# Hybrid mLSTM / Hyena / attention trunk: up projections accumulated over a bank that ScalarE filled, and adaLN chunks moved between engines and stages

## The chip, the cores and the metric

One NeuronCore of a Trainium2 chip runs the whole program once. The metric is the device time of one execution in microseconds (us), as the median of several runs. Engines are named as in the profile: PE is TensorE's matmul, PEld its weight load, DVE is VectorE, ACT is ScalarE, POOL is GpSimd, SP is the engine whose queue issues nearly all DMAs.

## What is computed

The reference is one inference step of a two-layer trunk on 512 latent tokens and 128 context tokens, D_MODEL = 1024, FF = 2816, float32. Cut to what the change touches:

```python
def adaln(cvec, w, b):                       # six chunks of 1024: shift, scale, gate; shift, scale, gate
    return jnp.split((jax.nn.silu(cvec) @ w + b)[:, None, :], 6, axis=-1)

def conv_ffn(h, w_up, w_conv, w_down):
    a, g = jnp.split(h @ w_up, 2, axis=-1)
    return (jax.nn.gelu(dwconv3(a, w_conv)) * g) @ w_down

for l in range(2):                           # l = 0: mixer A + B; l = 1: mixer C (attention)
    sh1, sc1, gt1, sh2, sc2, gt2 = adaln(c, w_ada[l], b_ada[l])
    x = x + gt1 * mixer(rmsnorm(x, g_mix[l]) * (1 + sc1) + sh1)
    x = x + gt2 * conv_ffn(rmsnorm(x, g_ffn[l]) * (1 + sc2) + sh2, w_up[l], w_conv[l], w_down[l])
```

Chunks are numbered 0 to 5 in the order of that list. Chunk 2 of a layer is first needed by the residual of its output projection, chunks 3 and 4 by the second norm, chunk 5 by the residual of its down projection.

## The kernel before

The activations lie transposed in SBUF, features on the 128 partitions and 640 tokens (512 latent, 128 context) along the free axis, as eight tiles of 128 features. A float32 matrix product is made of three fp32r matmuls: each operand is split into a high part (an ACT copy) and a low part (a DVE subtraction). The 640 tokens go in two halves of 320 (HT). So every weight that is loaded (a `raw` tile, four slots) costs an ACT copy and a DVE subtraction before PE can use it (`load_w` and `split_w`, lines 99 to 112; `split_half`, line 512).

The order of the stages is mixer A and B (`mixer_ab`), the output projection of layer 0 (`out_proj`, line 1152) with the second norm hidden in its last three tiles, the feed-forward network of layer 0 (`ffn_s`, line 414), mixer C (`mixer_c`, line 1179), the output projection of layer 1, its feed-forward network, and a last norm. A scheduler in the framework fixes the order of each engine's queue at compile time from its own model of times; at run time each queue is in order. `tc.issue_after(ins)` puts instructions behind a named one on its engine.

**The feed-forward network.** Chunks f = 0 to 2 of the 22 chunks of 128 features go through a plain product. From f = 3 on, `up(f)` (line 528) forms both halves of the up projection with seven products of a Winograd form instead of eight. Each product is 12 matmuls of 320 columns over four k-tiles; their weights are called w1 to w7 in the code. The seven products collect in three PSUM banks A, B and C: w1 then w2 in A; w6, w7, w4 in B; w5, w3 in C. The product w1 is needed by four results: once in A itself, and three times added to B. For this, ACT copies A to an SBUF tile `s1` (line 538), and three times DVE adds `s1` to B on its way out, to `u2`, `u3` and `gg`. Two chunks overlap: PE's order is w1 of the new chunk, w4 of the old one, w6 of the new, w3 of the old, then w2, w7, w5 of the new. After up(5), up(10) and up(15) a down projection (`down`, line 585) of the chunks up to then is made: eight output tiles, each with its weight split and with a residual in three pieces on DVE (line 360). The last down projection follows at the end.

**The adaLN chunks.** There are two ways to make one. `ada_pe` (line 212) makes a chunk, or two halves, on PE: four steps, each with two DMAs of 512 KB and 4 fp32 matmuls of 32 x 512 packed beside each other in the array (8 instructions in the trace), then one ACT copy, 4 tiny fp32 products with `selc` (8 instructions), and two DVE additions. `ada_dve` (line 242) makes it on DVE: 16 steps, each with a DMA of 256 KB (`adw`) and two multiply-and-sum instructions (`adj`, line 254), each followed by a read of the accumulator; at the end two small additions. Before the change layer 0's chunks 0 and 1 are made by `ada_pe` at the start, 2 to 5 by `ada_pe` in mixer A and B, one step after each of 16 projection tiles. Layer 1's chunks 0, 1, 2 are made by `ada_dve` in the feed-forward network of layer 0: the `filler` of `down` issues two steps after each output tile, with two `adw` buffers, so the 48 steps fill the first three down projections. Layer 1's chunks 3, 4, 5 are made by `ada_dve` in mixer C, six steps in each of the eight head pairs, with one `adw` buffer.

Of the kernel before, what the change touches and what calls it, by code (L numbers as in the profile page):

```python
# [17 lines left out]
P = 128  # L18
D = 1024
KT = 8  # L20
# [17 lines left out]
def trunk(ctx: ExitStack, tc: tile.TileContext, I, O, dbg=None, stop=None):  # L38
# [173 lines left out]
    def ada_pe(l, blocks, pl, tag, bufs, sbp, sbt):  # L212
        nm = "".join(f"{ch}{half}" for ch, half in blocks)
        pt = pst(f"ada{nm}")
        for kp in range(4):
            rr = [pl.tile([P, 1024], F32, tag=tag, name=f"wa{nm}{kp}{i}", bufs=bufs) for i in range(2)]
            for i, (ch, half) in enumerate(blocks):
                sp.dma_start(out=rr[i], in_=I["w_ada"][ch, kp, half])
            for par in range(2):
                for i in range(2):  # L220
                    j = 2 * par + i
                    pe.matmul(pt[32 * j : 32 * j + 32, :], cs_[0][:, 2 * kp + par, :],  # L222
                              rr[i][:, par * 512 : (par + 1) * 512], start=(kp == 0), stop=(kp == 3))
            if kp < 3:
                yield
# [16 lines left out]
    def ada_dve(l, ch, pl, bufs, cb):  # L242
# [20 lines left out]
        return [lambda k=k, h=h: step(k, h) for k in range(KT) for h in range(2)]  # L263

# [149 lines left out]
    def ffn_s(l, pools, early, steps, mk_hook):  # L414
# [7 lines left out]
        def filler(st=None):  # L422
            every[0] += 1
            st = steps if st is None else st
            for _ in range(2):
# [102 lines left out]
        def up(f):  # L528
# [8 lines left out]
            s1 = fp.tile([P, HT], F32, tag="s1", name=f"s1{l}_{f}")  # L537
            act.copy(out=s1, in_=A[:, :HT])
# [5 lines left out]
            B = pst(f"B{l}_{f}")  # L544
            product(B, split_half(a11, f"w6{f}"), T2, True, True)
            u2 = fp.tile([P, HT], F32, tag="u2", name=f"u2{l}_{f}")
            tt(u2, B[:, :HT], s1, ALU.add)
# [8 lines left out]
            tt(u3, B[:, :HT], s1, ALU.add)  # L556
# [7 lines left out]
            tt(gg[:, 0:HT], B[:, :HT], s1, ALU.add)  # L564
# [28 lines left out]
        for f in range(NC, NF):  # L593
# [5 lines left out]
            filler(early)  # L599
# [116 lines left out]
    def mixer_ab():  # L716
        with ExitStack() as es:
            es_h = es.enter_context(ExitStack())
            csil = es_h.enter_context(tc.tile_pool(name="cs", bufs=1, side="right")).tile([P, KT, 32], F32, name="csil")
            dve.memset(csil, 0.0)  # L720
            act.activation(out=csil[:, :, 0:2], in_=cond.rearrange("p s k -> p k s"), func=AF.Silu)
            cs_.append(csil)
# [77 lines left out]
            steps = [ada_pe(0, ((ch, 0), (ch, 1)), hw, "adr", 2, modp, "adasb") for ch in (2, 3, 4, 5)]  # L800
# [351 lines left out]
    def out_proj(l, src, order, hook, steps):  # L1152
        here = [None]

        def done(i, pt, a):
            here[0] = residual(l, 2, i, pt, a)

        def filler():
            for _ in range(2):
                if steps:  # L1160
                    with tc.issue_after(here[0]):
                        steps.pop(0)()

        ks = [(k, XH[:, k], XL[:, k]) for k in order]
        n = 0
        if psum["shape"] != (3, 2):
            linear([src[0], src[1]], done, f"oq{l}", ks=ks, by_half=False, filler=filler)
# [11 lines left out]
    def mixer_c():  # L1179
        with ExitStack() as es:  # L1180
# [3 lines left out]
            steps = [q for ch in (3, 4, 5) for q in ada_dve(1, ch, at, 1, cb)]  # L1184
# [112 lines left out]
            def pair_att(pr, nxt):  # L1297
# [118 lines left out]
    def layer(l, src, order, mk_hook):  # L1416
        with ExitStack() as es:
            pools = ffn_open(es, l)
            early, steps = [], []
            if l == 0:  # L1420
                cb = cond_bcast(pools[0], "cb0")
                steps = [q for ch in (0, 1, 2) for q in ada_dve(1, ch, pools[1], 2, cb)]
            with ExitStack() as en:
                nrm = en.enter_context(tc.tile_pool(name=f"nrm{l}1", bufs=2, side="right", reuse_waits="tile"))
                st = norm_steps(l, 1, nrm, pools[3])
                out_proj(l, src, order, lambda: next(st), early)
# [9 lines left out]
            ffn_s(l, pools, early, steps, hook)  # L1436
# [89 lines left out]
def pack(i):  # L1526
# [12 lines left out]
    o["w_ada"] = wa[0].reshape(4, 2, P, 6, 2, 512).transpose(3, 0, 4, 2, 1, 5).reshape(6, 4, 2, P, 1024)  # L1539
# [88 lines left out]
```

## Time and profile before

| | |
|---|---|
| runs of the kernel before | 1722.22, 1720.52, 1723.1 us; median 1722.22 us |
| the profiled execution's own time | 1722.28 us |
| its span, first to last instruction | 1720.5 us |
| mean granted TensorE clock | 0.987 of full speed |
| PE, DVE, ACT busy | 1642.9, 1300.1, 803.7 us |

The profiled execution lies 0.06 us from the median, and 1.8 us of its time lie outside its span. Busy time of PE is modelled from pipelined matmuls; idle time is listed by what ended it. A granted clock of 1.00 means 2.4 GHz, and 0.5 would mean 1.2 GHz throughout.

### The profile page before, as it was taken

How to read it: one execution, taken by the hardware profiler on the slowest of the kernel's cores; microseconds unless marked ns; L12 is line 12 of the kernel's file. 1: busy time of each engine (PE TensorE's matmuls, PEld its weight loads, DVE VectorE, ACT ScalarE, POOL GpSimd, SP SyncE). 2: the span in 40 equal slices, each digit the busy share in tenths (PEclk: the TensorE clock that was granted, in tenths of full speed). 3: DMA queues.
4: the chain of work that ended last, by engine and by line, in shares of the span. 5: the costliest groups of instructions: out<-in, count | busy, mean ns of one | idle time of the engine just before them, and what ended most of it. 6: DMA issues, size and time to landing. Idle time of an engine off the chain costs nothing.

```text
span 1720.5 us, 28571 instructions
## 1 busy us (share of the span) xinstructions
PE 1642.9 (95%) x11018; PEld 1541.3 (90%) x11018; DVE 1300.1 (76%) x2796; ACT 803.7 (47%) x1529; POOL 141.1 (8%) x158
## 2 busy tenths in 40 slices
PE   5999999999998999989998999999999999999997
PEld 2699778999998998989998889888999999999997
DVE  5887537665888989899857877778478597786974
ACT  6323226574751533425436555556266344443542
POOL 3110001000100000000020212111010000000001
PEclk9999999999999999999999999999999999999998
DMA  8334432132235333252323333332214232223221
GB/s 326 113 129 174 161 134 79 52 107 73 75 91 161 96 112 125 80 166 81 104 81 102 109 118 96 121 95 83 74 45 115 67 98 74 86 68 105 74 86 62
DMA packets 70136, 180.64 MB, mean 105 GB/s; under 512 B 8992, under 2 KB 19536, under 8 KB 69744
## 3 DMA queue, kind: packets, MB, share of 16 engines
q1 hardware_dynamic: 68176, 174.71, 33.0%
q0 software_dynamic: 1824, 4.10, 1.3%
q8 instruction: 87, 1.43, 0.3%
q14 instruction: 49, 0.40, 0.1%
HBM read 170.65 MB, written 4.20 MB: 102 GB/s over the span
## 4 chain that ended last, share of the span: by engine, by line
PE 53%; DVE 12%; DMA 5%; ACT 2%; issue 2%; POOL 0%; POOLq 0%; ACTq 0%; DVEq 0%
PE B L525 11%; PE pd L127 10%; PE C L525 7%; PE A L525 7%; DMA adw<-in_w_adaT 5%; PE pqk L127 4%; DVE adj L254 4%; PE pu L127 2%; PE pu L121 1%; PE pop L127 1%; PE pd L121 1%; PE pS L1329 1%; DVE s L1215 1%; PE py L1344 1%; PE pS L1309 1%
## 5 line engine op out<-in xcount | busy, mean ns | idle before, releaser
L360 DVE SCALAR_TENSOR_TENSOR x<-pd,mod,x 128x320 f32<-128x320 f32 (+2 forms) x192 | 75.0, 434 | 98.6 <-PE pd L127 89.0
L254 DVE CUSTOM_DVE_ANT_0 adj<-adw,cbc 128x512 bf16<-128x512 f32 x96 | 68.9, 718 | 22.8 <-DMA adw<-in_w_adaT 21.8
L254 DVE CUSTOM_DVE_ANT_0 adj<-adw,cb 128x512 bf16<-128x512 f32 x96 | 65.9, 687 | 10.5 <-DMA adw<-in_w_adaT 9.6
L575 DVE SCALAR_TENSOR_TENSOR fcb<-fca,cwf,fcb 128x641 f32<-128x641 f32 x76 | 67.0, 881 | 2.9 <-ACT fcb L573 2.6
L1331 ACT COPY pTs<-pS 128x384 f32<-128x384 f32 (+1 forms) x80 | 34.4, 434 | 36.4 <-PE pS L1329 36.0
L1317 DVE CUSTOM_DVE_ANT_0 s<-pS,bm 128x384 f32<-128x384 f32 x64 | 33.9, 548 | 18.8 <-PE pS L1316 18.6
L447 ACT ACTIVATE fcb<-fcb 128x641 f32<-128x641 f32 x44 | 32.6, 740 | 30.0 <-DVE fcb L575 30.0
L1329 PE MATMUL pS<-ident,s 128*128 128x128 f32 x208 | 36.9, 280 | 9.6 <-DVE s L1215 9.6
L530 DVE TENSOR_TENSOR u<-B,s 128x320 f32<-128x320 f32 x76 | 36.9, 486 | 12.1 <-PE B L525 11.6
L573 ACT ACTIVATE fcb<-fca,cwf 128x641 f32<-128x641 f32 x38 | 31.7, 834 | 27.3 <-DVE fca L530 26.8
L442 ACT CAST G<-gg 128x640 fp32r<-128x640 f32 x44 | 32.0, 727 | 26.5 <-DVE gg L530 22.1
L1215 DVE TENSOR_SCALAR s<-s,nm 128x384 f32<-128x384 f32 (+1 forms) x80 | 43.6, 548 | 0.8
L1213 ACT ACTIVATE s<-s,nm 128x384 f32<-128x384 f32 x64 | 39.1, 611 | 10.3 <-DVE nm L1317 9.8
L360 DVE SCALAR_TENSOR_TENSOR x<-pop,mod,x 128x320 f32<-128x320 f32 (+2 forms) x36 | 14.3, 433 | 36.7 <-PE pop L127 26.1
L288 ACT ACTIVATE sqn<-x 128x320 f32<-128x320 f32 x56 | 25.3, 466 | 33.8 <-DVE x L360 26.6
L222 PE MATMUL ada<-wa,csil 128*32 128x512 f32 x192 | 39.3, 653 | 1.5 <-DMA wa<-in_w_ada 1.3
L1394 POOL TENSOR_TENSOR fo<-fo,rs 128x320 f32<-128x320 f32 x8 | 6.9, 888 | 394.6 <-ACT rs L1386 394.6
L1329 PEld LDWEIGHTS pS<-ident,s 128*128 128x128 f32 x208 | 24.0, 141 | 16.3 <-DVE s L1215 12.3
L1292 POOL TENSOR_TENSOR bm<-amask,wr 128x768 f32<-128x768 f32 x14 | 28.7, 2052 | 115.0 <-issue 91.5
L443 DVE TENSOR_TENSOR G<-gg,G 128x640 fp32r<-128x640 f32 x44 | 36.0, 818 | 2.4 <-ACT G L442 2.3
L289 DVE TENSOR_TENSOR accn<-accn,sqn 128x320 f32<-128x320 f32 x56 | 30.7, 554 | 8.5 <-ACT sqn L288 7.6
L103 POOL TENSOR_TENSOR qk00l<-qk,qk00h 128x1024 fp32r<-128x1024 f32 x1 | 2.7, 2742 | 412.1 <-DVE rn L303 412.1
(2011 smaller groups left out, 6152.9 us busy)
## 6 DMA issues: line engine op xcount, KB each, us to landing
wa<-in_w_ada SPq DMA_DIRECT2D x48, 512.0 KB, 4.6
adw<-in_w_adaT SPq DMA_DIRECT2D x96, 256.0 KB, 3.0
d<-in_w_down SPq DMA_DIRECT2D x48, 320.0 KB, 2.9
qk<-in_w_qkv SPq DMA_DIRECT2D x24, 512.0 KB, 3.6
d<-in_w_down SPq DMA_DIRECT2D x16, 448.0 KB, 3.3
u<-in_w_up SPq DMA_DIRECT2D x12, 512.0 KB, 3.6
qk<-in_w_ab SPq DMA_DIRECT2D x8, 512.0 KB, 4.4
op<-in_w_oab SPq DMA_DIRECT2D x6, 512.0 KB, 3.7
```

Of the source, the lines that this page charges most:

```text
L121: pe.matmul(o, ww[:, kt], xx[:, c], start=False, stop=last and n == 1)
L127: pe.matmul(bank(pt, a)[:, : sp_[a][1] - sp_[a][0]], ww[:, kt], xx[:, slice(*sp_[a])], start=(first and n == 0), stop=(last and n == 2))
L222: pe.matmul(pt[32 * j : 32 * j + 32, :], cs_[0][:, 2 * kp + par, :], rr[i][:, par * 512 : (par + 1) * 512], start=(kp == 0), stop=(kp == 3))
L254: dve.tensor_tensor_reduce(out=jk, in0=w, in1=cb[:, s, c], op0=ALU.mult, op1=ALU.add, scale=1.0, scalar=0.0, accum_out=got[0][:, k, h, s : ...
L360: r = dve.scalar_tensor_tensor(out=x[:, k, c0:c1], in0=bank(pt, h)[:, c0 - h * HT : c1 - h * HT], scalar=mod[:, l, ch, k, s : s + 1], in1= ...
L443: here[0] = dve.tensor_tensor(out=g[:, 1], in0=pr, in1=g[:, 0].bitcast(F32), op=ALU.subtract).ins
L525: pe.matmul(o, ww[:, k], xx[:, k], start=(first and k == 0 and n == 0), stop=(last and k == 3 and n == 2), skip_group_check=not first)
L530: tt = lambda o, a, b, op: dve.tensor_tensor(out=o, in0=a, in1=b, op=op)
L575: dve.scalar_tensor_tensor(out=o, in0=av[:, d : d + T + 1], scalar=w[j], in1=o, op0=ALU.mult, op1=ALU.add)
L1213: act.activation(out=s, in_=src, func=AF.Exp, scale=-1.0, bias=nm, accum_out=sm)
L1215: return dve.tensor_scalar(out=s, in0=s, scalar1=sm, scalar2=None, op0=ALU.mult).ins
L1329: pe.transpose(pS[:, j * P : (j + 1) * P], s[:, j * P : (j + 1) * P], ident)
```

## The change

Three things are changed. In `up`, ACT copies the first product from bank A to bank B instead of to SBUF; the product w6 then accumulates over it, and the three results of B leave as plain ACT copies where DVE added `s1` before. Chunk 5 of each layer is made by `ada_pe` between the tiles of its own output projection (with a small `csil` tile of its own: a DVE memset and an ACT Silu; four buffers for the weights), so layer 0's mixer has three `ada_pe` chunks and 12 steps left. Of layer 1's other chunks, 0 and 1 stay in the feed-forward network of layer 0, now 32 steps, issued two and one in turn after each output tile; 2, 3 and 4 are made in mixer C, seven steps in each of the pairs 1 to 7 and none in pair 0.

```diff
 def ada_pe(l, blocks, pl, tag, bufs, sbp, sbt):
-                sp.dma_start(out=rr[i], in_=I["w_ada"][ch, kp, half])
+                sp.dma_start(out=rr[i], in_=I["w_ada"][6 * l if l else ch, kp, half])
...
+    def silu_cols(pl, nm):
+        csil = pl.tile([P, KT, 32], F32, name=nm)
+        dve.memset(csil, 0.0)
+        act.activation(out=csil[:, :, 0:2], in_=cond.rearrange("p s k -> p k s"), func=AF.Silu)
+        cs_[:] = [csil]
...
     def ffn_s(...): filler
-            for _ in range(2):
+            for _ in range(1 + every[0] % 2):
...
     def up(f):
             A = pst(f"A{l}_{f}")
             product(A, split_half(a11, f"w1{f}"), B11, True, True)
-            s1 = fp.tile([P, HT], F32, tag="s1", name=f"s1{l}_{f}")
-            act.copy(out=s1, in_=A[:, :HT])
+            B = pst(f"B{l}_{f}")
+            act.copy(out=B[:, :HT], in_=A[:, :HT])
...
-            B = pst(f"B{l}_{f}")
-            product(B, split_half(a11, f"w6{f}"), T2, True, True)
+            product(B, split_half(a11, f"w6{f}"), T2, False, True)
-            tt(u2, B[:, :HT], s1, ALU.add)
+            act.copy(out=u2, in_=B[:, :HT])
...
-            tt(u3, B[:, :HT], s1, ALU.add)
+            act.copy(out=u3, in_=B[:, :HT])
...
-            tt(gg[:, 0:HT], B[:, :HT], s1, ALU.add)
+            act.copy(out=gg[:, 0:HT], in_=B[:, :HT])
...
     def mixer_ab():
-            steps = [ada_pe(0, ((ch, 0), (ch, 1)), hw, "adr", 2, modp, "adasb") for ch in (2, 3, 4, 5)]
+            steps = [ada_pe(0, ((ch, 0), (ch, 1)), hw, "adr", 2, modp, "adasb") for ch in (2, 3, 4)]
...
             def qk_tile(j):
-                if j in (5, 3, 2, 6):
-                    filler()
...
-    def out_proj(l, src, order, hook, steps):
+    def out_proj(l, src, order, hook, ao):
+        st = ada_pe(l, ((5, 0), (5, 1)), ao, "adr", 4, ao, "adasb")
...
             use_psum(3, 2)
             n = 2
+        next(st)
         linear([src[i] for i in range(n, KT)], lambda i, pt, a: done(n + i, pt, a), f"op{l}",
-               ks=ks, head=0 if n else 3, tail=3, by_half=False, hook=hook, filler=filler)
+               ks=ks, head=0 if n else 3, tail=3, by_half=False, hook=hook, filler=lambda: next(st, 0))
...
     def mixer_c():
-            steps = [q for ch in (3, 4, 5) for q in ada_dve(1, ch, at, 1, cb)]
+            steps = [q for ch in (2, 3, 4) for q in ada_dve(1, ch, at, 1, cb)]
...
-                        if 1 <= n <= 6:
+                        if pr and 1 <= n <= 7 and steps:
...
     def layer(l, src, order, mk_hook):
-                steps = [q for ch in (0, 1, 2) for q in ada_dve(1, ch, pools[1], 2, cb)]
+                steps = [q for ch in (0, 1) for q in ada_dve(1, ch, pools[1], 2, cb)]
...
+                ao = en.enter_context(tc.tile_pool(name=f"ao{l}", bufs=1, side="right", reuse_waits="tile"))
+                silu_cols(ao, f"csil{l}")
```

## Rows read from the trace of the kernel before

**Rows 1.** The page, part 1: busy time, share of the span, instructions.
```profile
PE 1642.9 (95%) x11018; PEld 1541.3 (90%) x11018; DVE 1300.1 (76%) x2796; ACT 803.7 (47%) x1529; POOL 141.1 (8%) x158
```

**Rows 2.** Two stretches: us; busy PE, PEld, DVE, ACT, POOL; clock; DMA; GB/s.
```profile
515.30:846.50 331.20, 316.47 (x2091) 313.16 (x2089) 302.04 (x653) 130.17 (x219) 0.00 (x0) 0.97 0.39 116
1348.11:1655.00 306.89, 306.89 (x2093) 306.73 (x2092) 243.68 (x454) 130.00 (x220) 0.00 (x0) 1.00 0.30 86
```

**Rows 3.** Waits of PE, stretch 515 to 853: us in total, times, longest.
```profile
PE B L525 <- ACT w45wh L517: 5.1, 1, 5.1
PE B L525 <- ACT w415wh L517: 4.4, 1, 4.4
PE B L525 <- ACT w611wh L517: 3.9, 1, 3.9
```

**Rows 4.** Timeline around the end of layer 0's first down projection: start, duration, what.
```profile
551.61 0.69 DVE L254 CUSTOM_DVE_ANT_0 adj<-adw,cb 128x512 bf16<-128x512 f32 x1 [0.64 <-DMA adw<-in_w_adaT]
...
559.19 0.62 ACT L517 CAST w45wh<-u_6a 128x512 fp32r<-128x512 f32 x1 [2.15 <-DVE u_6a L530]
...
559.86 0.90 PE L525 MATMUL B<-TT,w45wh 128*128 128x320 f32 x2 [5.09 <-ACT w45wh L517]
...
560.29 0.68 DVE L254 CUSTOM_DVE_ANT_0 adj<-adw,cb 128x512 bf16<-128x512 f32 x1
```

**Rows 5.** Groups by line, stretch 515 to 852: busy us, mean ns | idle before.
```profile
L254 DVE CUSTOM_DVE_ANT_0 adj<-adw,cb 128x512 bf16<-128x512 f32 x96 | 65.9, 687 | 10.5 <-DMA adw<-in_w_adaT 9.6
L254 DVE DVE_READ_ACCUMULATOR2_ANT ada<- 128x1 f32 x96 | 7.8, 82 | 0.0
```

**Rows 6.** Timeline of SP's queue in layer 0's first down projection.
```profile
522.87 1.79 SPq L251 DMA_DIRECT2D adw<-in_w_adaT  x2
...
553.55 5.36 SPq L251 DMA_DIRECT2D adw<-in_w_adaT  x3
```

**Rows 7.** The page, part 5: the additions that bring s1 to u2 and u3.
```profile
L530 DVE TENSOR_TENSOR u<-B,s 128x320 f32<-128x320 f32 x76 | 36.9, 486 | 12.1 <-PE B L525 11.6
```

**Rows 8.** Groups by line, stretch 1348 to 1655: the copy of the first product.
```profile
L538 ACT COPY s<-A 128x320 f32<-128x320 f32 x16 | 6.8, 424 | 1.4 <-PE A L525 0.9
```

**Rows 9.** Timeline: first product's copy and the next products, chunks 7 and 14, layer 1.
```profile
1397.39 0.46 PE L525 MATMUL B<-TT,w17wh 128*128 128x320 f32 x2
...
1397.64 0.42 ACT L538 COPY s<-A 128x320 f32<-128x320 f32 x1
...
1399.15 0.46 PE L525 MATMUL B<-TT,w67wh 128*128 128x320 f32 x2
...
1519.49 0.42 ACT L538 COPY s<-A 128x320 f32<-128x320 f32 x1
...
1520.62 0.46 PE L525 MATMUL B<-TT,w413wh 128*128 128x320 f32 x2
```

**Rows 10.** PE in mixer A and B: one adaLN step, and the products with selc.
```profile
103.67 1.06 PE L222 MATMUL ada<-wa,csil 128*32 128x512 f32 x8
...
135.94 0.95 PE L230 MATMUL adaq<-selc,adasb 128*128 128x4 f32 x8
```

**Rows 11.** Stretch 100 to 240, the tile ada alone; columns PE, PEld, DVE, ACT.
```profile
100.00:240.00 140.00, 24.32 (x128) 3.43 (x128) 0.00 (x0) 2.14 (x4) 1.00 0.48 164
```

**Rows 12.** Timeline at layer 1's output projection: ACT's gap and PE's.
```profile
1216.29 1.05 ACT L102 CAST op11h<-op 128x1024 fp32r<-128x1024 f32 x1 [4.66 <-PE poq L127]
...
1220.13 0.52 PE L127 MATMUL pop<-XH,op10h 128*128 128x320 f32 x2 [2.70 <-DVE mod L258]
```

**Rows 13.** Timeline at layer 0's output projection: last split, PE's wait, a table load.
```profile
384.25 0.83 DVE L1175 TENSOR_TENSOR XL<-og,XH 128x640 fp32r<-128x640 f32 x1 [0.79 <-ACT XH L1174]
...
388.83 0.54 PE L127 MATMUL pop<-XH,op00h 128*128 128x320 f32 x2 [0.44 <-DVE x L360]
...
389.26 1.28 ACT L268 ACT_TABLE_LOAD   x1
```

**Rows 14.** The page, part 6: the chunk's DMAs on PE's way: count, KB, median us.
```profile
wa<-in_w_ada SPq DMA_DIRECT2D x48, 512.0 KB, 4.6
```

More of the change, by code (lines that the diff above doesn't have):

```diff
@@ L212, in ada_pe @@
     def ada_pe(l, blocks, pl, tag, bufs, sbp, sbt):
-        nm = "".join(f"{ch}{half}" for ch, half in blocks)
+        nm = str(l) + "".join(f"{ch}{half}" for ch, half in blocks)
         pt = pst(f"ada{nm}")
@@ L412, in ffn_open, with ffn_s @@
         return fc, fp, gtile, keep
-    def ffn_s(l, pools, early, steps, mk_hook):
+    def ffn_s(l, pools, steps, mk_hook):
         fc, fp, gtile, keep = pools
@@ L420, in ffn_s, with filler @@
         every = [0]
-        def filler(st=None):
+        def filler():
             every[0] += 1
-            st = steps if st is None else st
-            for _ in range(2):
+            st = steps
+            for _ in range(1 + every[0] % 2):
                 if st:
@@ L598, in ffn_s @@
                     next(s_)
-            filler(early)
             old = new
@@ L718, in mixer_ab @@
             es_h = es.enter_context(ExitStack())
[L719 to L722, printed above, removed]
+            silu_cols(es_h.enter_context(tc.tile_pool(name="cs", bufs=1, side="right")), "csil")
             modp = es.enter_context(tc.tile_pool(name="modp", bufs=1))
@@ L1150, in mixer_ab @@
             dump("ym", og)
-    def out_proj(l, src, order, hook, steps):
[L1153 to L1162, printed above, removed]
+    def out_proj(l, src, order, hook, ao):
+        st = ada_pe(l, ((5, 0), (5, 1)), ao, "adr", 4, ao, "adasb")
+        done = lambda i, pt, a: residual(l, 2, i, pt, a)
         ks = [(k, XH[:, k], XL[:, k]) for k in order]
@@ L1166, in out_proj @@
         if psum["shape"] != (3, 2):
-            linear([src[0], src[1]], done, f"oq{l}", ks=ks, by_half=False, filler=filler)
+            linear([src[0], src[1]], done, f"oq{l}", ks=ks, by_half=False)
             use_psum(3, 2)
             n = 2
+        next(st)
         linear([src[i] for i in range(n, KT)], lambda i, pt, a: done(n + i, pt, a), f"op{l}",
-               ks=ks, head=0 if n else 3, tail=3, by_half=False, hook=hook, filler=filler)
+               ks=ks, head=0 if n else 3, tail=3, by_half=False, hook=hook, filler=lambda: next(st, 0))
     def split_y(y, k):
@@ L1418, in layer @@
             pools = ffn_open(es, l)
-            early, steps = [], []
+            steps = []
             if l == 0:
                 cb = cond_bcast(pools[0], "cb0")
-                steps = [q for ch in (0, 1, 2) for q in ada_dve(1, ch, pools[1], 2, cb)]
+                steps = [q for ch in (0, 1) for q in ada_dve(1, ch, pools[1], 2, cb)]
             with ExitStack() as en:
@@ L1425, in layer @@
                 st = norm_steps(l, 1, nrm, pools[3])
-                out_proj(l, src, order, lambda: next(st), early)
+                ao = en.enter_context(tc.tile_pool(name=f"ao{l}", bufs=1, side="right", reuse_waits="tile"))
+                silu_cols(ao, f"csil{l}")
+                out_proj(l, src, order, lambda: next(st), ao)
                 list(st)
@@ L1434, in hook @@
                 return lambda: next(rest[0])
-            ffn_s(l, pools, early, steps, hook)
+            ffn_s(l, pools, steps, hook)
             list(rest[0])
@@ L1538, in pack @@
     wa = i["w_ada"]
-    o["w_ada"] = wa[0].reshape(4, 2, P, 6, 2, 512).transpose(3, 0, 4, 2, 1, 5).reshape(6, 4, 2, P, 1024)
+    wr = wa.reshape(2, 4, 2, P, 6, 2, 512).transpose(0, 4, 1, 5, 3, 2, 6).reshape(12, 4, 2, P, 1024)
+    o["w_ada"] = wr[[0, 1, 2, 3, 4, 5, 11]]
     o["w_adaT"] = wa.reshape(2, D, 6, KT, P).transpose(0, 2, 3, 4, 1).reshape(12, KT, P, D)[5:]
```

## The prediction

> **What bounds the kernel now.** I read the page first. PE is busy for 1642.9 us, 95% of the span, and DVE comes next with 76% [rows 1]. So nothing that only frees DVE or ACT can pay, unless PE stands still or runs slowly somewhere because of them. The kernel has one good test for that: the two feed-forward networks hold the same matmuls, one with adaLN steps on DVE beside it (layer 0) and one without (layer 1). The second view therefore cuts out the same part of both, from the first matmul of the first down projection to the last product of the up projections [rows 2]. It has 2091 and 2093 matmuls. Layer 1 takes 306.89 us, with PE busy all the time and the clock at 1.00; layer 0 takes 331.20 us. The difference of 24.3 us is all that can be won there. It has two parts. PE is idle for 331.20 - 316.47 = 14.7 us, and it is busy for 316.47 - 306.89 = 9.6 us longer on the same work, with a granted clock of 0.97. In layer 1 every microsecond is PE's own work, so there DVE's relief is worth nothing.
>
> The third view, the waits, gives the place: three waits of 5.1, 4.4 and 3.9 us, 13.4 in all, each by the first product that follows one of the three down projections, for a weight split [rows 3]. The fourth, the timeline around the first of them, gives the reason [rows 4]. PE's down projection began at 515.30 and is 240 matmuls long; at 306.89 / 2093 = 0.147 us each it ends at about 550.5. From 551.61 to 560.29 DVE still works off 8 `adj` instructions of the adaLN steps that came with the last output tiles, among the sums that the next weights are made from; ACT's cast of w4 waits for such a sum, and PE waits 5.1 us for the cast. SP's queue shows why the steps lag: it issues the `adw` loads in pairs, six pairs in 553.55 - 522.87 = 30.7 us, so 5.1 us a pair [rows 6]. Eight pairs need 41 us, and the down projection lasts only 35.2.
>
> **Part 1, fewer adaLN steps beside layer 0's down projections.** They go from 16, 16, 16 to 12, 12, 8. DVE loses a third of 65.9 + 7.8 us [rows 5], 24.6 us. More to the point, 12 steps are 6 pairs, 30.7 us, under the 35.2 us of PE's work. With the first step at about 521, as now, the last ends near 553, so that some 2 `adj` are left after PE's end instead of 8. Six fewer, of 0.69 us [rows 5], are 4.1 us off a wait of 5.1; up to 1.0 us stays in the first two waits, and nothing in the third, where 8 steps are long done. Part 2 takes a little more off DVE there, so I leave 1.4 us in all. The slow clock came after these waits, and I count its 9.6 us as gone with them. That is 13.4 - 1.4 + 9.6 = 21.6 us won. Bounds: 24.3 us if layer 0 becomes like layer 1; 14 us if one of the three restarts, (13.4 + 9.6) / 3 = 7.7 us each, stays as it is.
>
> **Part 2, the first product copied into bank B.** DVE loses three additions in each of 38 chunks, 114 x 0.486 = 55 us [rows 7], and ACT gains 114 copies of about 0.424 us, 48 us [rows 8] (its one copy of A stays and gets another target, for which the trace has no row). Neither is on PE's path in the steady state, since layer 1 shows PE full with DVE at 244 and ACT at 130 of 307 us [rows 2]. But a wait is new: w6 may start only when the copy has filled B, and every later product is queued behind it on PE. The cover is the old chunk's w4, which stands between. In chunk 7 of layer 1, w4 starts at 1397.39, the copy ends at 1398.06, and w6 starts at 1399.15, so 1.09 us are to spare; in chunk 14, where the copy starts late, it ends at 1519.91 and w6 starts at 1520.62, with 0.71 us to spare [rows 9]. Most chunks look like the first of these. In chunk 3 of either layer there is no old chunk: w6 then waits those 1398.06 - 1397.39 = 0.67 us, 1.3 us for two layers. For the other chunks I take 0 and keep 3 us as upper bound, some tenths in a few of them; the case in which all are late is a rival below. The ACT copies out of B gate w7, w4 and later bank uses; two products (some 3.5 us) lie between, eight times a copy's length.
>
> **Part 3, layer 1's chunk 5 on PE.** Four steps of 1.06 and the small products of 0.95 us [rows 10] are 5.2 us on an engine that is full in the output projection. Lower bound: the wait of 2.70 us that PE has there before the third tile [rows 12] takes some of it, 5.2 - 2.7 = 2.5. Upper bound: the price in mixer A and B, 24.32 us for four chunks [rows 11], so 6.1 + 0.95 = 7.0. I take 5.2, since between the tiles the eight instructions come together as in the row.
>
> **Part 4, layer 0's chunk 5 from mixer A and B to the output projection.** PE saves 5.2 to 7.0 us in the first place and spends 5.2 in the second. Its 8 loads of 512 KB now stand on SP's queue among those of the projection's weights and of the first up weights. If their SBUF space is freed only by the last split, which ends at 384.25 + 0.83 = 385.08 [rows 13], the first lands 4.6 us later [rows 14], at 389.7, while PE reached the third tile at 388.83 [rows 13]: 0.9 us of waiting, and up to 9.6 / 3 = 3.2 us if the clock falls. So -1.8 to +4.1; I take 0. The DVE and ACT instructions of the chunk are five small ones and hide.
>
> **Part 5, mixer C.** It has 48 steps before and after; pair 0 loses six and the others have seven instead of six. What DVE does late at its end delays the residual that PE waits 2.70 us for [rows 12]; with a denser row of steps it may be somewhat later. I take 0, bounds -1 and +3.
>
> **Part 6, the Silu of layer 1.** The memset and the Silu stand at the end of mixer C. A table load took 1.28 us [rows 13], and ACT is idle for 4.66 us there [rows 12], which hides it. If the queue has it between softmax steps, two switches come on a path that PE waits for, 2 x 1.28 = 2.6 us; that is a bound. The Trainium skill ("ScalarE: Activation LUTs", What ACT_TABLE_LOAD costs) gives 2.66 us for each switch, with a drain after the load; by it the same case would cost 5.3 us, and in the gap still nothing. The row shows the load alone.
>
> **Sum.** -21.6 + 1.3 + 5.2 + 0 + 0 + 0 = -15.1 us, made against the profiled execution's own 1722.28 us, which is the median within 0.1: 1707.2 us. With the bounds that may well come together, this case reaches from 1698 to 1715.
>
> **The rivals.** (a) *The stall stays.* The steps are issued behind the residual of each tile; if the queues are laid out so that the last steps again stand ahead of the sums for the next weights, two of three restarts stay, 15.4 us, and the time is 1722.6, no change. For it: the loads' pace of 5.1 us a pair leaves only 4.5 us of slack in a down projection. Against: the third has 8 steps only. (b) *Both output projections stall.* A wait like the 2.70 us [rows 12] for the chunk's loads in each layer, with 3.2 us of slow clock, 11.8 us together: 1719.0. For it: PE's queue is in order, and the loads take 4.6 us. Against: SP can issue layer 1's loads early. (c) *The fill is late, and it gets slower.* ACT's queue is in order; if the copy into B stands behind casts of 0.62 us [rows 4] and copies that wait for PE, each w6 waits. The point from which it decides is 15.1 / 38 = 0.40 us per chunk, so a copy some 1.5 us later than now. At 2.0 us later, 0.9 x 38 = 34 us: 1741. For it: 48 us more on ACT. Against: ACT would be busy for 151 of 307 us in a stretch like that of layer 1 (130 plus 51 copies of 0.42), and its copy has a start close to the product's end now.
>
> **How the numbers follow.** The forecast has 0.71, (a) 0.11, (b) 0.08, (c) 0.10. A difference of 0.2%, 3.4 us, is about what a measurement of this kernel can tell from no change. Forecast, half of (b) and a part of (a), in which only one restart stays, are faster: 0.79. The rest of (a) and (b) is within 0.2%: 0.10. Case (c) and a remainder are slower: 0.11. The range of 1698 to 1719 takes in the forecast's own range and (b), and leaves out most of (a) and (c).
>
> **What would show it.** Right: in the same stretch as [rows 2] layer 0 within 3 us of layer 1, clock 1.00; no wait of over 1.5 us by a first product after a down projection; the last `adj` of the first down projection before 555; layer 1's stretch as long as before; the output projection of layer 1 about 5 us longer. Wrong: waits of PE for ACT's copy into B in many chunks, layer 1's stretch longer, waits for `wa` loads in the output projections, or `adj` still behind the end of the down projections.

## The result, and the profile after

The changed kernel takes 1703.42 us (median of 4 runs, 1701.24 to 1704.26) where the kernel before takes 1722.66 (1720.52 to 1726.52) beside it: a ratio of 0.9884 [0.9864, 0.9904], 19.2 us less. The forecast was 1707.2, 15.1 us less, with a range of 1698 to 1719. The profiled execution has a span of 1699.5 us against 1720.5.

The page of the changed kernel, part 1 (busy time, share of the span, instructions), answers to [rows 1]:

```profile
PE 1628.2 (96%) x11058; PEld 1534.2 (90%) x11058; DVE 1241.9 (73%) x2620; ACT 846.4 (50%) x1647; POOL 142.0 (8%) x158
```

DVE has lost 58 us, ACT has gained 43, and PE is busy for 15 us less although it has 40 matmuls more. So most of the gain is not idle time that closed but the same work done in less time on PE.

For "where", the span is cut at places that both traces have: the first and the last matmul of a tile on PE (the first piece begins with the span). The stretch of [rows 2] is one of the pieces. "Chunk 3" is the piece from the first product of the up projections to the first matmul of the first down projection.

| stage (us, from first and last matmuls in the timelines) | before | after | change |
|---|---|---|---|
| start, mixer A and B, to the output projection | 365.28 | 345.66 | -19.6 |
| output projection, layer 0, from its third tile | 45.21 | 52.07 | +6.9 |
| plain up chunks, layer 0 | 47.38 | 47.40 | 0.0 |
| chunk 3, layer 0 | 33.88 | 39.79 | +5.9 |
| stretch of [rows 2], layer 0 | 331.36 | 307.46 | -23.9 |
| mixer C | 288.15 | 290.38 | +2.2 |
| output projection, layer 1: first tiles, wait, the rest | 79.93 | 83.17 | +3.2 |
| plain up chunks, layer 1 | 47.34 | 47.34 | 0.0 |
| chunk 3, layer 1 | 33.89 | 38.56 | +4.7 |
| stretch of [rows 2], layer 1 | 306.92 | 307.31 | +0.4 |

These make -20.2; the last down projections and the tail bring the rest of the span's -21.0. The total came near the forecast, but two lines that the forecast held near zero did not: mixer A and B won far more, and chunk 3 lost 10.6 us in the two layers.

The two stretches again, in the changed kernel (columns as in [rows 2]: us; busy PE, PEld, DVE, ACT, POOL; clock; DMA; GB/s):

```profile
508.46:815.92 307.46, 306.95 (x2092) 306.48 (x2091) 267.01 (x538) 148.08 (x269) 0.00 (x0) 1.00 0.38 111
1327.43:1634.74 307.31, 307.31 (x2097) 307.27 (x2096) 227.08 (x405) 148.30 (x269) 0.00 (x0) 1.00 0.30 86
```

Layer 0 is now as long as layer 1, at a clock of 1.00 and with 0.5 us of PE idle. The end of its first down projection, timeline of the changed kernel (start, duration, what), answers to [rows 4]:

```profile
543.66 0.31 PE L531 MATMUL A<-XH,w55wh 128*128 128x320 f32 x1
...
544.01 0.68 DVE L254 CUSTOM_DVE_ANT_0 adj<-adw,cb 128x512 bf16<-128x512 f32 x1
...
545.89 0.69 DVE L254 CUSTOM_DVE_ANT_0 adj<-adw,cb 128x512 bf16<-128x512 f32 x1
...
547.12 0.69 DVE L254 CUSTOM_DVE_ANT_0 adj<-adw,cb 128x512 bf16<-128x512 f32 x1
547.23 0.62 ACT L523 CAST w45wh<-u_6a 128x512 fp32r<-128x512 f32 x1 [0.22 <-DVE u_6a L536]
...
547.91 0.55 PE L531 MATMUL B<-TT,w45wh 128*128 128x320 f32 x2
```

The last `adj` starts 38.7 us into the stretch, where it was 45.0 before, and PE's product follows its cast without a wait. Three `adj` still start after the down projection, whose last matmul stands just ahead of the one at 543.66. They cost nothing, because PE has other products for the next 4 us, whose weights are ready; the cast ends at 547.85 and its product starts at 547.91, so it is just in time. In place of the three waits of [rows 3], the waits of PE from the output projection on read:

```profile
PE pS L1320 <- DVE s L1206: 14.3, 18, 1.3
PE C L531 <- DMA XL<-keep: 7.8, 2, 4.5
...
PE C L531 <- DVE gg L536: 0.5, 1, 0.5
```

The second line is new (none in the kernel before), and it is chunk 3. The timeline there, layer 0 (the halves of a weight go by the name of their buffer, so `B<-TT,w13wh` is w6):

```profile
468.21 1.29 POOL L479 DMA_DIRECT2D XL<-keep  x1 [5.81 <-ACT XL L478]
...
470.43 0.31 PE L531 MATMUL C<-XH,w53wh 128*128 128x320 f32 x1
470.63 0.41 ACT L544 COPY B<-A 128x320 f32<-128x320 f32 x1
...
475.27 0.41 PE L531 MATMUL C<-XL,w53wh 128*128 128x320 f32 x1 [4.53 <-DMA XL<-keep]
...
475.66 0.56 PE L531 MATMUL B<-TT,w13wh 128*128 128x320 f32 x2
476.02 0.47 PE L531 MATMUL B<-TT,w13wl 128*128 128x320 f32 x1
```

After w1, PE's queue holds the first three matmuls of w5 (bank C), then w6. The second of the three reads the low part of an input that POOL's accumulating DMA makes; it was issued at 468.21 and lands at 475.2. The fill of B is done at 471.04, so w6, with its inputs ready, stands for 4.6 us behind a product that nobody needs yet. In the kernel before, w6 comes straight after w1 in this chunk. The price is more than the wait, as three windows of 20 us show (columns as above):

```profile
440.00:460.00 20.00, 18.46 (x124) 17.88 (x123) 18.48 (x26) 16.23 (x24) 0.91 (x1) 1.00 0.36 86
460.00:480.00 20.00, 15.47 (x96) 15.21 (x95) 12.90 (x22) 10.62 (x16) 2.18 (x2) 0.91 0.46 93
480.00:500.00 20.00, 20.00 (x138) 20.00 (x138) 15.11 (x26) 11.24 (x23) 0.00 (x0) 1.00 0.31 86
```

The granted clock is 0.91 in the window with the wait, and 0.50 (1.2 GHz) in the part of it from 475.9 to 479.2: the matmuls there come 0.27 us apart instead of 0.15.

Last, mixer A and B. Some of the adaLN steps among the last q/k tiles in PE's timeline, first of the kernel before, then of the changed one:

```profile
191.99 1.04 PE L222 MATMUL ada<-wa,csil 128*32 128x512 f32 x2
193.90 1.06 PE L222 MATMUL ada<-wa,csil 128*32 128x512 f32 x6
199.75 1.04 PE L222 MATMUL ada<-wa,csil 128*32 128x512 f32 x2 [1.08 <-DMA wa<-in_w_ada]
201.65 1.06 PE L222 MATMUL ada<-wa,csil 128*32 128x512 f32 x6
```

```profile
192.55 1.07 PE L222 MATMUL ada<-wa,csil 128*32 128x512 f32 x8
200.78 1.06 PE L222 MATMUL ada<-wa,csil 128*32 128x512 f32 x8
```

A step in two groups costs 1.04 + 1.06 us, nearly twice as much as in one. The tile `ada` alone, 186 to 243 us, before and after (us; PE, PEld, DVE, ACT; clock; DMA; GB/s):

```profile
186.00:243.00 57.00, 15.79 (x64) 2.17 (x64) 0.00 (x0) 1.17 (x2) 1.00 0.55 185
```

```profile
186.00:243.00 57.00, 3.20 (x24) 0.47 (x24) 0.00 (x0) 0.58 (x1) 1.00 0.38 121
```

Before, eight steps, seven of them in two groups, took 15.79 us, 1.97 each; now three take 3.20, 1.07 each. So the time of [rows 11] was not four chunks at the same price: the first eight steps cost 8.5 of the 24.32 us, the last eight 15.8.

### The profile page after: what moved, and what is told of

Read it like the earlier page. It is cut to its first block, busy times and chain, and to the rows that moved or that the text cites. A ratio compares the mean times of both kernels' runs of the same rounds, so it can differ in the third digit from the quotient of the medians.

```text
span 1699.5 us, 28588 instructions
## 1 busy us (share of the span) xinstructions
PE 1628.2 (96%) x11058; PEld 1534.2 (90%) x11058; DVE 1241.9 (73%) x2620; ACT 846.4 (50%) x1647; POOL 142.0 (8%) x158
## 4 chain that ended last, share of the span: by engine, by line
PE 83%; DVE 9%; DMA 3%; ACT 3%; issue 2%; POOL 0%; SPq 0%; POOLq 0%; ACTq 0%; DVEq 0%
PE pd L127 15%; PE B L531 12%; PE pqk L127 8%; PE C L531 8%; PE A L531 8%; PE pop L127 3%; PE px L127 2%; PE phyb L127 2%; PE po L127 2%; PE ada L222 2%; DMA adw<-in_w_adaT 2%; PE pop L121 1%; PE pu L121 1%; PE pd L121 1%; PE pS L1320 1%
## 5 line engine op out<-in xcount | busy, mean ns | idle before, releaser
L254 DVE CUSTOM_DVE_ANT_0 adj<-adw,cbc 128x512 bf16<-128x512 f32 x96 | 67.9, 708 | 35.5 <-DMA adw<-in_w_adaT 34.5
L1320 PE MATMUL pS<-ident,s 128*128 128x128 f32 x208 | 36.4, 280 | 14.3 <-DVE s L1206 14.3
L366 DVE SCALAR_TENSOR_TENSOR x<-pop,mod,x 128x320 f32<-128x320 f32 (+2 forms) x36 | 14.3, 433 | 43.9 <-PE pop L127 31.1
L254 DVE CUSTOM_DVE_ANT_0 adj<-adw,cb 128x512 bf16<-128x512 f32 x64 | 44.0, 687 | 1.8 <-DMA adw<-in_w_adaT 0.9
L294 ACT ACTIVATE sqn<-x 128x320 f32<-128x320 f32 x56 | 25.3, 466 | 37.7 <-DVE x L366 33.6
L536 DVE TENSOR_TENSOR gg<-gg,fcb 128x512 f32<-128x512 f32 x76 | 33.9, 488 | 10.8 <-ACT fcb L453 10.8
```

Of the source, the lines that this page charges most:

```text
L254: dve.tensor_tensor_reduce(out=jk, in0=w, in1=cb[:, s, c], op0=ALU.mult, op1=ALU.add, scale=1.0, scalar=0.0, accum_out=got[0][:, k, h, s : ...
L366: r = dve.scalar_tensor_tensor(out=x[:, k, c0:c1], in0=bank(pt, h)[:, c0 - h * HT : c1 - h * HT], scalar=mod[:, l, ch, k, s : s + 1], in1= ...
L1320: pe.transpose(pS[:, j * P : (j + 1) * P], s[:, j * P : (j + 1) * P], ident)
```

## The experiments

The medians of the kernel before were 1718.34 beside E1 to E4, 1719.14 beside E5 to E8, 1719.99 beside E9 and 1719.03 beside E10 and E11, so each is given as its change against the one beside it (the changed kernel: -19.2). The totals in the expectations are absolute and start from 1722.66 or 1703.42, so a total 3 or 4 us under its range need not speak against a theory; E1, E2 and E6 end 3, 1 and 1 us under it. The stages named are those of the table above.

**E1, the fill alone.** The kernel before with part 2 of the change and nothing of the moved adaLN steps.

```diff
-            s1 = fp.tile([P, HT], F32, tag="s1", name=f"s1{l}_{f}")
-            act.copy(out=s1, in_=A[:, :HT])
+            B = pst(f"B{l}_{f}")
+            act.copy(out=B[:, :HT], in_=A[:, :HT])
...
-            product(B, split_half(a11, f"w6{f}"), T2, True, True)
+            product(B, split_half(a11, f"w6{f}"), T2, False, True)
-            tt(u2, B[:, :HT], s1, ALU.add)
+            act.copy(out=u2, in_=B[:, :HT])
... (u3 and gg alike)
```

> The kernel before with the second part alone: the first product is copied into bank B, the three results of B leave as ACT copies; all adaLN chunks stay as before. Theory (the fewer adaLN steps remove the restart stalls, the fill does not): layer 0's stretch from the first down projection to the last product stays at 322 to 331 us (331.2 before), since 8 adj still stand behind each down projection; layer 1's stays at 307; chunk 3 of both layers has the new wait for the DMA-made low part of T1, some 5 us each. Total 1724 to 1733 us. Rival (DVE relief by the fill is what removed the stalls): layer 0's stretch falls to 312 us or less, total 1708 to 1714 us.

Measured: 1721.11 us, a ratio of 1.0014 [1.0002, 1.0026], +2.8 us. Its layer 0 stretch and the waits in it:

```profile
513.10:836.30 323.20, 313.97 (x2097) 311.45 (x2097) 285.86 (x605) 147.40 (x269) 0.00 (x0) 0.98 0.38 118
```

```profile
PE B L525 <- ACT w45wh L517: 3.7, 1, 3.7
PE B L525 <- ACT w415wh L517: 2.7, 1, 2.7
PE B L525 <- DVE w611wl L518: 1.8, 1, 1.8
PE B L525 <- ACT w611wh L517: 1.0, 1, 1.0
...
```

The relief of DVE takes 8 us off the stretch (331.4 to 323.1) and leaves all three restarts, each shorter. Chunk 3 gives 9.8 back (33.88 to 38.57 in layer 0, 33.89 to 38.99 in layer 1, with the same wait for `XL<-keep`). The fill by itself wins nothing.

**E2, the moved steps alone.** The changed kernel with the up projections of the kernel before.

```diff
-            B = pst(f"B{l}_{f}")
-            act.copy(out=B[:, :HT], in_=A[:, :HT])
+            s1 = fp.tile([P, HT], F32, tag="s1", name=f"s1{l}_{f}")
+            act.copy(out=s1, in_=A[:, :HT])
...
-            product(B, split_half(a11, f"w6{f}"), T2, False, True)
+            B = pst(f"B{l}_{f}")
+            product(B, split_half(a11, f"w6{f}"), T2, True, True)
... (u2, u3 and gg as DVE additions again)
```

> The changed kernel with the up projections as before (s1 in SBUF, three DVE additions); all moves of adaLN chunks kept. Theory: layer 0's stretch is 307 to 312 us, mixer A and B as short as in the changed kernel, no wait in chunk 3 of either layer (first product to first down projection 33.9 us instead of 39.8 and 38.6). Total 1703.4 - 10.6 + 0 to 4 = 1693 to 1697 us. Rival (both parts are needed for the restarts): the stretch stays above 318 us, total above 1702 us.

Measured: 1692.02 us, 0.9841 [0.982, 0.9861], -26.3 us: better than the whole change. The stretch of layer 0 is 308.07 us, chunk 3 33.89 and 33.91. So the moved steps alone bring 23.3 of the 23.9 us in the stretch; beside them the fill adds 0.6 there, where it took 8 us off alone, and it loses 10.6 in chunk 3.

**E3, w5 of chunk 3 behind w6.** The changed kernel; only the order of issue in the one chunk differs (`product` now returns its last instruction).

```diff
...
-            product(B, split_half(a11, f"w6{f}"), T2, False, True)
+            w6 = product(B, split_half(a11, f"w6{f}"), T2, False, True)
...
-            product(C, split_half(ss, f"w5{f}"), T1, True, True)
+            hs = split_half(ss, f"w5{f}")
+            with tc.issue_after(w6) if f == NC else ExitStack():
+                product(C, hs, T1, True, True)
```

> The changed kernel, with the product w5 of chunk 3 alone kept behind w6 on TensorE's queue. Theory (the wait in chunk 3 is one of order: w5 was put ahead of w6 because w6 has to wait for the fill, and met a DMA that lands 4.5 us later): the wait of 4.5 and 3.3 us is gone, chunk 3 keeps the 0.7 us of its fill; first product to first down projection 34.5 us in both layers; total 1703.4 - 10.6 + 1.3 = 1694 us (1692 to 1697). Rival (the wait comes back at the next product that reads T1 or at the fill): total 1700 us or more.

Measured: 1693.01 us, 0.9845 [0.9825, 0.9865], -25.3 us. Chunk 3 takes 34.25 us in both layers. Its timeline in layer 0:

```profile
473.19 0.41 ACT L545 COPY B<-A 128x320 f32<-128x320 f32 x1
...
473.66 0.56 PE L531 MATMUL B<-TT,w13wh 128*128 128x320 f32 x2 [0.50 <-ACT B L545]
```

That is the wait that the forecast had priced, 0.50 us, and the stage is 0.36 us longer than before. With the fill and the dependency unchanged, the order alone was worth 5.5 and 4.3 us. The medians show 6.1 of these 9.8 us; E3's profiled execution has 2.6 us more in mixer A and B and 1.5 in layer 1's plain up chunks, in code that the edit doesn't touch; such differences stand between executions of one kernel too (last section).

**E4, chunk 3 in the old way.** The changed kernel, without the fill in chunk 3 only.

```diff
+            fill = f > NC
+            if fill:
+                B = pst(f"B{l}_{f}")
+                act.copy(out=B[:, :HT], in_=A[:, :HT])
+            else:
+                s1 = fp.tile([P, HT], F32, tag="s1", name=f"s1{l}_{f}", bufs=1)
+                act.copy(out=s1, in_=A[:, :HT])
...
-            product(B, split_half(a11, f"w6{f}"), T2, False, True)
+            if not fill:
+                B = pst(f"B{l}_{f}")
+            product(B, split_half(a11, f"w6{f}"), T2, not fill, True)
... (u2, u3 and gg by DVE additions where there is no fill)
```

> The changed kernel, with chunk 3 of each layer alone made in the old way (s1 in SBUF, DVE additions), all others by the fill. Theory (order): no wait for T1's DMA in chunk 3, first product to first down projection 33.9 us in both layers, total 1692 to 1695 us, 0 to 2 us below the kernel with w5 held back. Rival (the fill delays later chunks too, so the wait only moves): total 1700 us or more.

Measured: 1694.35 us, 0.9856 [0.9832, 0.988], -24.0 us; chunk 3 33.90 and 33.88. The total is 1.3 us above E3's, where the theory had it 0 to 2 us below; the intervals of the two overlap. It agrees with E3: the loss came from what the fill did to the order in the chunk that has no older chunk beside it, and not from the other chunks.

**E5, two steps per tile again.** The changed kernel with the old pace beside the first two down projections, so the same 32 steps stand 16, 16 instead of 12, 12, 8.

```diff
-            for _ in range(1 + every[0] % 2):
+            for _ in range(2):
```

> The changed kernel with two adaLN steps after every tile of layer 0's down projections instead of two and one in turn; still 32 steps, so the first two down projections have 16 each, as before the change, and the third none. Theory (it is the pace of the steps against the loads that makes a restart late): the first two restarts stall again, by less than before since the fill relieves DVE (the fill alone left 16 us over three restarts); layer 0's stretch 315 to 320 us instead of 307.5, total 1711 to 1716 us. Rival (the number of steps, one third less work on DVE, is what counts): stretch at most 310 us, total 1702 to 1706 us.

Measured: 1712.86 us, 0.9963 [0.995, 0.9977], -6.3 us. The stretch of layer 0, and its two longest waits:

```profile
512.30:831.60 319.30, 312.62 (x2092) 310.42 (x2091) 266.33 (x539) 147.70 (x269) 0.00 (x0) 0.98 0.35 107
```

```profile
PE B L531 <- ACT w45wh L523: 3.4, 1, 3.4
PE B L531 <- ACT w611wh L523: 1.9, 1, 1.9
```

DVE does the same work as in the changed kernel (266.33 against 267.01 us), and 11.8 of the 23.9 us are gone: two restarts are back, the third stage has no steps and no restart. What counts is how many steps stand beside one down projection, as the pace of [rows 6] says.

**E6, layer 0's chunk 5 back in mixer A and B.** The changed kernel with four chunks there as before, none under layer 0's output projection.

```diff
-            steps = [ada_pe(0, ((ch, 0), (ch, 1)), hw, "adr", 2, modp, "adasb") for ch in (2, 3, 4)]
+            steps = [ada_pe(0, ((ch, 0), (ch, 1)), hw, "adr", 2, modp, "adasb") for ch in (2, 3, 4, 5)]
...
+                if j in (5, 3, 2, 6):
+                    filler()
...
-        st = ada_pe(l, ((5, 0), (5, 1)), ao, "adr", 4, ao, "adasb")
+        st = ada_pe(l, ((5, 0), (5, 1)), ao, "adr", 4, ao, "adasb") if l else iter(())
...
-        next(st)
+        next(st, 0)
```

> The changed kernel with layer 0's chunk 5 back in mixer A and B, with the four extra steps beside its last projection tiles, and none in layer 0's output projection. Theory (there a step costs nearly double, since its eight instructions run in two groups, and the chunk before suffers too): mixer A and B up to the third tile of the output projection 388 us instead of 369 to 371, the output projection 6.9 us shorter, total 1703.4 + 10 to 12 = 1713 to 1716 us. Rival (a chunk costs the same 5 to 7 us in either place, and the rest of the difference was chance): total 1702 to 1705 us.

Measured: 1711.63 us, 0.9963 [0.9946, 0.9979], -7.5 us. Mixer A and B takes 362.01 us (+16.4 against the changed kernel), the output projection 45.20 (-6.9). The theory had 388 us up to the third tile; it comes at 385.56. So this move alone is worth 9.5 us.

**E7, the same twelve steps, placed close together.** The changed kernel; no step beside the four Hyena tiles, two beside each of the last four q/k tiles. The work is the same.

```diff
+                if j in (5, 3, 2, 6):
+                    filler()
...
-                linear(W(i), lambda _, pt, a: done_h(i, pt, a), f"hyb{i}", head=0, filler=filler)
+                linear(W(i), lambda _, pt, a: done_h(i, pt, a), f"hyb{i}", head=0)
```

> The changed kernel with the same 12 adaLN steps in mixer A and B, but none beside the four Hyena tiles and two each beside the last four q/k tiles, so that work is the same and only the density of the steps differs. Theory (two steps per tile outrun the two weight buffers, so that a step's two loads come apart and its matmuls run in two groups of about 1 us each): mixer A and B 8 to 13 us longer, total 1711 to 1717 us. Rival (it was the fourth chunk's own work): mixer A and B as in the changed kernel within 2 us, total 1702 to 1706 us.

Measured: 1711.87 us, 0.9959 [0.9945, 0.9972], -7.3 us. Mixer A and B takes 357.64 us, 12.0 more than in the changed kernel. Steps among the last q/k tiles:

```profile
191.66 1.05 PE L222 MATMUL ada<-wa,csil 128*32 128x512 f32 x2 [1.87 <-DMA wa<-in_w_ada]
193.56 1.06 PE L222 MATMUL ada<-wa,csil 128*32 128x512 f32 x6
```

The split steps of the kernel before are back, with its wait for `wa`. So the larger part of the saving in mixer A and B, 12.0 of 16.9 us (the start of the program left out, see below), is not that of a removed chunk: it comes from one step per tile instead of two. What is left, 4.9 us, is near the 5.2 that the forecast had for the chunk itself. That the loads, with two buffers, are what splits a step fits the waits for `wa`, but no run gave them more buffers, so this part is argued; a step is split in both output projections of the changed kernel too, and there the loads have four.

**E8 and E11, the moves with six steps per pair in mixer C.** E2, with mixer C's 48 steps laid out as before (six in each of the eight pairs). E11 is the same kernel again.

```diff
-                        if pr and 1 <= n <= 7 and steps:
+                        if 1 <= n <= 6 and steps:
```

> The kernel with the adaLN moves alone (up projections as before, 1692.0 us), and in mixer C six steps in each of the eight pairs, as before the change, instead of seven in the last seven. Theory (the denser steps are why mixer C takes 293.2 us instead of 288.2): mixer C 287 to 290 us, total 1687 to 1690 us. Rival (the longer mixer C is another order of its queues, not the density): mixer C stays above 291 us, total 1690 to 1694 us.

> The kernel without the fill (adaLN moves alone, six steps per pair) once more, beside the one with it on the same chip. Theory (the fill is worth nothing once the order in chunk 3 is right): median within 2 us of the kernel with the fill; mixer C 286 to 290 us in either. Rival: 2.5 us or more above it.

Measured: 1688.34 us, 0.982 [0.9798, 0.9841], -30.8 us, and again 1686.48, 0.9816 [0.9798, 0.9834], -32.5. Groups of mixer C's steps, changed kernel and then E8 (busy us, mean ns | idle before):

```profile
L254 DVE CUSTOM_DVE_ANT_0 adj<-adw,cbc 128x512 bf16<-128x512 f32 x96 | 67.9, 708 | 35.5 <-DMA adw<-in_w_adaT 34.5
```

```profile
L254 DVE CUSTOM_DVE_ANT_0 adj<-adw,cbc 128x512 bf16<-128x512 f32 x96 | 69.1, 720 | 20.3 <-DMA adw<-in_w_adaT 19.3
```

With seven steps per pair DVE waits 15 us longer for the steps' loads, in order, ahead of the softmax steps behind them, and PE's wait for `s` is 14.3 us against 9.2 in E8. E2, which differs from E8 by this edit alone, has 35.5 us of such waits on DVE as well, and 13.3 on PE. Over the profiles, mixer C takes 290.5 us on average with seven (7 kernels, 288.6 to 293.3) and 287.3 with six (6 profiles, 285.1 to 289.5). Layer 1's output projection is shorter too, and there the two groups do not overlap: 80.8 us with six steps in E8 to E11, 82.3 to 83.2 with seven in all seven kernels. PE's timeline of E8 ahead of the third tile of that projection:

```profile
1183.17 1.92 PE L222 MATMUL ada<-wa,csil 128*32 128x512 f32 x16
1185.02 0.56 PE L127 MATMUL pop<-XH,op10h 128*128 128x320 f32 x2
```

Two whole adaLN steps of chunk 5 stand there without a wait, 1.92 us together; in the changed kernel the second of them waited for its load and was split (rows in the next section).

**E9 and E10, the fill in the right order with six steps per pair.** E3 with the edit of E8. E10 is the same kernel again, on one chip with E11.

> The changed kernel with both corrections: w5 of chunk 3 kept behind w6, and six adaLN steps in each of mixer C's eight pairs. It differs from the fastest kernel so far (adaLN moves alone with six steps per pair, 1688.3 us) by the fill of bank B alone. Theory (once the order in chunk 3 is right the fill is worth nothing, since TensorE is full with or without it): 1687 to 1691 us, each stage within 2 us of that kernel. Rival (the relief of DVE still pays somewhere): below 1686 us. Rival (the fill costs in steady state): above 1692 us.

> The fastest kernel so far (fill with w5 of chunk 3 behind w6, six steps per pair) once more, beside the kernel without the fill on the same chip. The queues of mixer C have the same order in both, yet one profiled execution of each gave 286.7 and 289.5 us there. Theory (that difference is the execution's): the two medians lie within 2 us of each other. Rival (the fill is worth about 3 us, 1685.0 against 1688.3): this one is 2.5 us or more below the other.

Measured: 1685.04 us, 0.9809 [0.9786, 0.9833], -35.0 us, and again 1685.31, 0.9805 [0.9786, 0.9824], -33.7. E9's total lies in the range of its rival that the relief of DVE still pays. E10 beside E11, which lacks the fill, is 1.2 us less, with intervals that overlap almost wholly, and the forecast of E10, within 2 us, holds. So either version is some 12 to 16 us faster than the changed kernel, by their changes against the kernel before, and whether the fill adds anything once the steps are moved can't be told from these runs.

The stages on which these readings rest, in us:

| stage | after | E1 | E2 | E3 | E5 | E6 | E7 | E8 | E9 |
|---|---|---|---|---|---|---|---|---|---|
| mixer A and B | 345.66 | 364.69 | 345.45 | 348.25 | 348.62 | 362.01 | 357.64 | 346.37 | 345.46 |
| output projection, layer 0 | 52.07 | 45.21 | 52.22 | 52.06 | 52.09 | 45.20 | 52.07 | 52.06 | 52.07 |
| chunk 3, layer 0 | 39.79 | 38.57 | 33.89 | 34.25 | 40.66 | 38.57 | 39.20 | 33.89 | 34.24 |
| stretch, layer 0 | 307.46 | 323.09 | 308.07 | 307.65 | 319.23 | 307.57 | 307.51 | 308.00 | 307.45 |
| mixer C | 290.38 | 286.69 | 293.23 | 289.22 | 288.55 | 293.29 | 289.17 | 289.51 | 286.71 |
| chunk 3, layer 1 | 38.56 | 38.99 | 33.91 | 34.25 | 38.59 | 38.57 | 37.02 | 33.91 | 34.24 |
| stretch, layer 1 | 307.31 | 307.31 | 306.91 | 307.24 | 307.23 | 307.23 | 307.23 | 306.90 | 307.23 |

## Why the prediction was right, and where it was not

**The direction and the main term were right.** Part 1 was put at -21.6 us and measured -23.3 (E2's stretch against that before), by the mechanism named: the three waits and the slow clock after them went, and nothing came in their place in that stretch. In the kernel before the granted clock was 0.50 from 559.2 to 565.9, as the first wait ended; in the changed kernel it was 1.00 over the whole stretch. E5 gives this saving to the number of steps beside one down projection. E2's stretch ended 1.2 us above layer 1's, where the forecast left 2.7, and the changed kernel's 0.2 above: the last `adj` came 38.7 us into the stretch, about where the forecast put it, but the 1.4 us of waiting left for it did not come. For this the forecast had misread the rows. The product that waits is not the first one after the down projection; PE has some 4 us of other products before it (in [rows 4] the wait begins at 554.77, the down projection ends at about 550.5). So `adj` behind the end of the down projection, named as a sign of being wrong, did show, and cost nothing.

**Part 2 failed, +10.4 us in place of +1.3:** 10.6 in chunk 3, 0.4 in layer 1's stretch, -0.6 in layer 0's. The step that failed is "in chunk 3 ... w6 then waits those 0.67 us". Its size was right: E3 shows 0.50 us of waiting, 0.36 on the stage. But it took PE's order as given, while the order of issue is laid out anew around the added dependency: the first matmuls of w5 went ahead of the waiting w6, and they waited for a DMA. The forecast's upper bound for this edit, 3 us, counted only lateness of the fill. The exchange of work was smaller than the 55 and 48 us that it had too: E1's page has DVE busy for 1260.3 us and ACT for 844.6, so DVE lost 39.8 and ACT gained 40.9. No time hung on that.

**Part 4 failed on the other side, -10.0 us in place of 0, and outside its bounds of -1.8 to +4.1.** Of the -19.6 us in mixer A and B, 2.75 are no effect of the change (last section), which leaves -16.9; the output projection of layer 0 cost 6.9 (the forecast's 5.2 with one step split in two). The step that failed is "PE saves 5.2 to 7.0 us in the first place". The 7.0 came from the mean of [rows 11] over four chunks. The mean hid that the last eight steps cost 15.8 of its 24.3 us because two stood beside each tile, and taking a chunk out thins the rest as well: E7 gets 12.0 us back without removing or adding a step. The forecast read the denser part only in one sum over the whole stretch; the timeline of that part, with its groups of two and six, would have shown it.

**Part 3 came out at +3.2 in place of 5.2,** inside its bounds of 2.5 to 7.0, but not for the reason of its value. The wait of [rows 12] took part of the work, as the lower bound has it, but with six steps per pair in mixer C more of it goes in: E8's projection is only 0.9 us longer than before, below the lower bound. That is 2.3 us less than the changed kernel's, and 1.6 less than that of E2, one edit apart. PE's timeline at that place in the changed kernel:

```profile
1188.27 1.06 PE L222 MATMUL ada<-wa,csil 128*32 128x512 f32 x8
1190.25 1.04 PE L222 MATMUL ada<-wa,csil 128*32 128x512 f32 x2 [0.92 <-DMA wa<-in_w_ada]
1191.79 0.53 PE L127 MATMUL pop<-XH,op10h 128*128 128x320 f32 x2 [0.49 <-DVE x L366]
...
1198.99 1.06 PE L222 MATMUL ada<-wa,csil 128*32 128x512 f32 x6
```

A step and a part of the next lie in the hole ahead of the third tile, where E8 has two whole steps. A 0.9 us wait for a load is the most that rival (b) came to.

**Part 5 was put at 0 with bounds of -1 and +3 and measured +2.2.** E8 to E11 show that the denser row of steps does cost time, about 3 us in mixer C by the means of the profiles, and the 1.6 to 2.3 us of the output projection come on top. So the value taken was wrong, and the upper bound, 3 us, was about met in mixer C alone. Most of it stands elsewhere than the forecast feared, at PE's waits for the softmax's `s`; ahead of the third tile PE waits 0.49 us for DVE, and in E8 not at all. **Part 6 was right.** ACT loads the table once, in its gap at the end of mixer C (timeline of the changed kernel):

```profile
1183.27 1.28 ACT L268 ACT_TABLE_LOAD   x1
1184.56 0.22 ACT L268 ACTIVATE csil<-cond 128x16 f32<-128x16 f32 x1
1187.20 1.05 ACT L102 CAST op11h<-op 128x1024 fp32r<-128x1024 f32 x1 [2.43 <-PE poq L127]
```

The Trainium skill ("ScalarE: Activation LUTs", What ACT_TABLE_LOAD costs) adds a drain to each load; here the activation starts 0.01 us after the load's 1.28 us, so the row shows the load alone.

**The rivals.** (a) was not seen in the changed kernel, but E5 is what it described: with 16 steps beside a down projection, two restarts stay, 11.8 us. (c) was not seen: layer 1's stretch is 0.4 us longer and no product there waits for the fill. **The total** landed 4 us from the forecast because two errors of opposite sign, +9.1 and -10.0, cancel; the range held for that reason as much as for its width.

## What to carry to other kernels

Where a scheduler lays out the order, price an added dependency with the work that may be moved in front of the waiting instruction, and look at what that work itself waits for. Don't price a removed step by the mean over a stretch: take the row at the place where it stood, and ask what its neighbours cost when it is gone. When an edit of several parts wins, run the parts apart: here one part won more alone than the whole, and a size that was changed without need, seven steps per pair, cost 4 to 5 us in two stages (E8 against E2, E9 against E3).

## What the runs showed of the hardware

The eight packed matmuls of an adaLN step take 1.06 us together; two of them alone take 1.04, six 1.06. So a split of such a step costs a whole step. Two whole steps back to back take 1.92 us (E8).

The clock at the start of the program differs between executions of the same instructions. Busy times of 20 to 60 us, kernel before and then the changed one (PE, PEld, DVE, ACT, POOL; clock; DMA; GB/s):

```profile
20.00:60.00 40.00, 35.05 (x164) 19.81 (x165) 26.51 (x66) 24.38 (x39) 13.22 (x8) 0.91 0.61 229
```

```profile
20.00:60.00 40.00, 36.01 (x179) 21.65 (x180) 30.32 (x73) 25.81 (x42) 13.46 (x8) 1.00 0.68 251
```

The granted clock is 0.91 or 1.00 there, and the first projection of the Hyena part starts at 48.86 or 46.11 us, 2.75 apart; it takes 44.86 us in both, and from its start on mixer A and B are 16.9 us shorter. E8 shows 1.00 and E11, the same kernel, 0.91, so it is not the change. Other stages differ between executions of one kernel as well: layer 0's plain up chunks take 47.40 us in E8 and 48.92 in E11 (with a granted clock of 0.50 from 459.7 to 462.9 in E11, and of 1.00 all through these chunks in E8), mixer C 289.51 and 287.93 in these two, 286.71 and 285.08 in E9 and E10. So the 3 us of E8 are read from thirteen profiles.

A wait of 4.5 us on PE made its stage 5.9 us longer: most of the 3.7 us behind it ran at half pace, with a granted clock of 0.50. Not each such wait brings that: in layer 1's chunk 3 the same wait of 3.3 us made the stage 4.7 us longer in the changed kernel, where the clock from 1280 to 1300 us was 0.91, and 3.1 in E7, where it was 1.00. [rows 2] show the slower pace on a larger scale, with 0.97 over layer 0's stretch.
